# A QKV projection on one core: first row tiles loaded and turned one at a time, and a reordered last pair

## The chip, the core and the metric

The kernel runs on one core of one Trainium2 chip. The metric is device time in microseconds (us) of one execution. A profile is taken of one execution; its own clock counts from the start of the span, and its span is about 1.8 us shorter than the time that is reported for the run.

In the views of the profile, PE is TensorE (PEld its loading of weights), ACT is ScalarE, DVE is VectorE, POOL is GpSimd and SP is SyncE; a q behind a name marks the part of the engine that issues transfers, and L141 is line 141 of that run's kernel. To turn rows is to transpose them, to cast them is to convert them to bf16.

The kernel before takes 362.96 us (median of six runs, 362.75 to 363.25, taken in the rounds of the changed kernel). Each later group of experiments has runs of the kernel before on the same chip; their medians lie between 362.75 and 362.89.

## The reference

```python
x = randn(16, 512, 768)          # float32: 8192 rows of 768
w_qkv = randn(768, 2304)
qkv = np.matmul(x, w_qkv)
q, k, v = qkv[..., :768], qkv[..., 768:1536], qkv[..., 1536:]
return np.stack([q, k, v], axis=0).astype(np.float32)   # 75.5 MB out
```

## The kernel before

A "pair" is two row tiles of 128 rows. There are 32 pairs. Pairs 3 to 31 are done by a scheme of seven products with sums of blocks (`do(u, 1)` to `do(u, 7)`) on two groups of 1024 columns, and directly on the 256 columns that remain (`rem`). The scheme needs sums of weight blocks, which aren't there at the start, so pairs 0 to 2 are done directly in bf16, block by block of 512 columns. For these the rows are cast, turned on TensorE (six 128 by 128 transposes a row tile) and copied back. The change touches this start and the last pair. Cuts are marked by `...`.

```python
def load_rows(p):                                   # one transfer of 768 KB for a pair
    xin[p] = xin_pool.tile([P, 2, K], fp32, name="xin")
    rows = x_flat[p * 2 * P:(p + 1) * 2 * P, :]
    nc.sync.dma_start(xin[p][:], rows.rearrange("(r m) k -> m r k", m=P))

def copy_halves(dst, src, two):                     # VectorE, and ScalarE where two
    ...
def cast_rows(p, two=True):                         # both rows of a pair to bf16
    src = xin.pop(p)
    xc[p] = s_pool.tile([P, 2, K], bf16, name="xc", tag="s")
    for r in range(2):
        halves = (slice(0, K // 2), slice(K // 2, K))
        copy_halves([xc[p][:, r, n] for n in halves], [src[:, r, n] for n in halves], two)
def turn_rows(p, two=True):                         # both rows of a pair
    ...
            for j in range(KT):
                nc.tensor.transpose(ps[:, j, :], cols[:, j, :], eye)
    ...
# the last pair, a and b being the two groups of columns
    do(a, 1); do(b, 1); do(a, 2); do(a, 6); do(b, 2); do(b, 6)     # (one to a line)
    ...
    do(b, 4)
    store_cols(b, 1, 0, CB, nc.scalar)
    for u in (a, b):
        do(u, 3)
        store_cols(u, 0, CB, 2 * CB, nc.sync)
    rem_stored(1)
# the start: the loads, all on SyncE's queue, in this order
load_rows(0)
...
load_rows(1)
load_blocks(0, 0, 1)                                # six weight blocks of 256 KB
st_rem = o_pool.tile([P, KT, REM], fp32, name="str", tag="o")
load_w(st_rem[:], 0, KT, R_OFF, REM)                # the remainder's weights
load_rows(2)
load_blocks(0, 1)
...
# the start: the work
busy(11)                                            # products of zeros, the warm-up
cast_rows(0)
turn_rows(0)
busy(4)
cast_rows(1)
cast_k(0)                                           # a weight block to bf16
cast_k(1)
turn_rows(1)
...
block(0, 0, b1[0], singles, nothing)                # 24 products, pairs 0 and 1
rem(0)
rem(1)
cast_rows(2, False)
turn_rows(2, False)
block(0, 0, b1[0], halves((4, 5)), nothing)         # 12 products, pair 2
```

## Time and profile before

| | kernel before |
|---|---|
| time, median of six runs | 362.96 us |
| span of the profiled run | 361.4 us |
| landings: first pair, second pair, third pair | 5.05, 7.03, 15.31 us |
| first real product | 9.19 us |
| first product of the next weight block | 20.54 us |
| one repeated pair | 10.74 us |
| TensorE's end, last landing | 356.87, 360.04 us |

TensorE is busy almost all of the span (353.3 of 361.4 us), so the reader should look at two things only: when dense products begin, and what follows the last of them. The middle is the same in both kernels. The prediction below shows the lines of the page, of the timeline at both ends and of three windows. This is the kernel before in windows of 1 us; in each line the last three numbers are the granted clock, the share of the 16 DMA engines' time that is busy, and GB/s.

```profile
4.00:5.00 1.00, 1.00 (x3) 0.30 (x2) 0.00 (x0) 0.00 (x0) 0.00 (x0) 1.00 1.01 406
6.00:7.00 1.00, 1.00 (x14) 0.91 (x13) 0.33 (x1) 0.01 (x1) 0.00 (x0) 1.00 1.03 400
```

In both windows the DMA engines are full (shares of 1.01 and 1.03), at 400 GB/s and more. (The clock column reads 1.00 also where the trace has no record of the clock. In this run the record gives full speed only from 6.43 us, so in the first microseconds the spacing of the products tells the clock, and this column does not.)

### The profile page before, as it was taken

To read this page: it belongs to the slowest core of one execution; us is meant where nothing else is said; L and a number is where in the kernel's file an instruction comes from. 1 tells how busy PE (TensorE), PEld (TensorE's weight loads), DVE (VectorE), ACT (ScalarE), POOL (GpSimd) and SP (SyncE) were. 2 spreads that over 40 slices of the span, in tenths; PEclk is the share of its full clock that TensorE was granted. 3 is DMA by queue.
4 is the path that set the end of the run, shared out by engine and by line. 5 is a ranking of instruction groups with operands and counts; after the bars stand their busy time and mean duration, and the time that the engine had idled before them with its cause. 6 is when DMAs were issued, how large, how long until landed. Compare 5 with 4: busy or idle time off the path is not lost.

```text
span 361.4 us, 5220 instructions
## 1 busy us (share of the span) xinstructions
PE 353.3 (98%) x1765; PEld 250.8 (69%) x1797; DVE 222.7 (62%) x239; ACT 182.5 (51%) x304; POOL 174.4 (48%) x180
## 2 busy tenths in 40 slices
PE   8999999999999999999999999999999999999994
PEld 3644577777777777777777777777777777777763
DVE  3489546666566765566675565676556676556642
ACT  4547555455454545454545444445545454545452
POOL 0000970566664445664445665444666444566410
PEclk9999999999999999999999999999999999999999
DMA  7999969799899989999999999898999998989766
GB/s 294 381 383 338 348 227 345 271 354 304 279 322 298 296 275 296 282 313 314 284 278 295 282 306 316 284 276 291 295 285 317 295 296 276 297 279 331 267 251 242
DMA packets 80617, 108.08 MB, mean 299 GB/s; under 512 B 4816, under 2 KB 60368, under 8 KB 80592
## 3 DMA queue, kind: packets, MB, share of 16 engines
q1 hardware_dynamic: 65184, 96.35, 82.3%
q10 hardware_dynamic: 15408, 11.41, 9.9%
q8 instruction: 14, 0.23, 0.3%
q14 instruction: 11, 0.09, 0.1%
HBM read 32.24 MB, written 75.50 MB: 298 GB/s over the span
## 4 chain that ended last, share of the span: by engine, by line
PE 96%; ACT 1%; issue 1%; ACTq 0%; DVE 0%
PE ps L206 75%; PE ps L256 11%; PE ps L382 9%; PE ps L362 1%; PE ps L161 1%; ACT o L237 0%; ACTq L297 0%; ACT xb L141 0%; ACT orem L311 0%; DVE xb L139 0%; ACT xc L141 0%; ACTq L313 0%; DVE zero L340 0%; ACTq L311 0%
## 5 line engine op out<-in xcount | busy, mean ns | idle before, releaser
L206 PE MATMUL ps<-t,s 128*128 128x512 f32 x696 | 173.8, 398 | 0.0
L206 PEld LDWEIGHTS ps<-t,s 128*128 128x128 f32 x696 | 130.7, 188 | 29.8
L169 POOL CAST xb<-xf 128x1536 bf16<-128x1536 f32 x29 | 46.4, 1601 | 167.7 <-DVE xf L124 167.7
L234 DVE TENSOR_TENSOR o<-o,ps 128x512 f32<-128x512 f32 x58 | 39.9, 688 | 87.6 <-ACT o L233 87.6
L124 DVE STREAM_TRANSPOSE xf<-xin 128x1536 f32<-128x1536 f32 x29 | 85.7, 2956 | 9.7 <-DMA xin<-in_x_dram 7.1
L206 PE MATMUL ps<-b,xb 128*128 128x512 bf16 x320 | 82.4, 380 | 1.5
L233 ACT ACTIVATE o<-ps 128x512 f32<-128x512 f32 x58 | 34.7, 598 | 44.3 <-PE ps L206 44.3
L206 PEld LDWEIGHTS <-xb 128*128 128x128 bf16 x348 | 31.7, 98 | 35.6 <-issue 7.6
L227 ACT ACTIVATE o<-ps 128x512 f32<-128x512 f32 x58 | 34.8, 600 | 40.0 <-PE ps L206 37.3
L240 DVE TENSOR_TENSOR o<-o,ps 128x512 f32<-128x512 f32 x58 | 39.9, 688 | 21.4 <-PE ps L206 20.2
L206 PE MATMUL ps<-b,s 128*128 128x512 f32 x174 | 48.7, 389 | 0.0
L256 PE MATMUL ps<-w_rem,xb 128*128 128x256 bf16 x384 | 47.2, 273 | 0.0
L237 ACT ACTIVATE o<-ps 128x512 f32<-128x512 f32 x58 | 34.7, 598 | 24.1 <-PE ps L206 21.3
L220 ACT ACTIVATE o<-ps 128x512 f32<-128x512 f32 x58 | 34.6, 597 | 23.8 <-DVE o L240 20.7
L256 PEld LDWEIGHTS <-xb 128*128 128x128 bf16 x384 | 37.4, 98 | 11.2 <-issue 0.5
L224 DVE TENSOR_TENSOR o<-o,ps 128x512 f32<-128x512 f32 x58 | 36.5, 673 | 3.4 <-PE ps L206 2.1
L206 PEld LDWEIGHTS ps<-b,s 128*128 128x128 f32 x174 | 32.7, 188 | 6.8
L178 POOL TENSOR_TENSOR s<-s,xf 128x384 fp32r<-128x384 f32 x29 | 29.5, 1016 | 2.3
L266 ACT ACTIVATE orem<-ps 128x512 f32<-128x512 f32 x31 | 18.6, 598 | 22.7 <-PE ps L256 21.4
L179 POOL TENSOR_TENSOR s<-xf 128x384 fp32r<-128x384 f32 x29 | 29.5, 1017 | 0.0
L181 POOL TENSOR_TENSOR s<-xf,s 128x384 fp32r<-128x384 f32 x29 | 29.4, 1015 | 0.0
L177 POOL TENSOR_TENSOR s<-xf 128x384 fp32r<-128x384 f32 x29 | 29.3, 1012 | 0.0
(36 smaller groups left out, 127.2 us busy)
## 6 DMA issues: line engine op xcount, KB each, us to landing
out_dram<-o SPq DMA_DIRECT2D x62, 768.0 KB, 5.1
out_dram<-o SPq DMA_DIRECT2D x65, 256.0 KB, 4.6
xin<-in_x_dram SPq DMA_DIRECT2D x62, 192.0 KB, 6.7
xin<-in_x_dram ACTq DMA_DIRECT2D x54, 192.0 KB, 4.5
out_dram<-orem SPq DMA_DIRECT2D x31, 256.0 KB, 5.5
st<-in_w_qkv_dram SPq DMA_DIRECT2D x6, 768.0 KB, 14.1
xin<-in_x_dram SPq DMA_DIRECT2D x3, 768.0 KB, 5.8
st<-in_w_qkv_dram SPq DMA_DIRECT2D x6, 256.0 KB, 6.3
```

Of the source, the lines that this page charges most:

```text
L124: nc.vector.transpose(t[:].rearrange("p j (g b) -> p g j b", b=G), xin.pop(p)[:].rearrange("p g (a j) -> p g j a", a=G),)
L169: nc.gpsimd.tensor_copy(out=xb[p][:], in_=xf[p][:])
L206: nc.tensor.matmul(ps[:], lhs[j], rhs[j], start=(start and j == 0), stop=(j == KH - 1), skip_group_check=True,)
L220: nc.scalar.activation(c11, u.x[:], ident)
L224: nc.vector.tensor_tensor(c11, c11, u.z[:], op=add)
L227: nc.scalar.activation(c12, u.x[:], ident)
L233: nc.scalar.activation(c22, u.x[:], ident)
L234: nc.vector.tensor_tensor(c22, c22, u.y[:], op=add)
L237: nc.scalar.activation(c21, u.x[:], ident)
L240: nc.vector.tensor_tensor(c12, c12, u.y[:], op=add)
L256: nc.tensor.matmul(ps, xb[p][:, j, r * P:(r + 1) * P], w_rem[:, j, :], start=(j == 0), stop=(j == KT - 1), skip_group_check=True,)
L382: nc.tensor.matmul(ps[n][:], xb[p][:, j, r * P:(r + 1) * P], w[:, j, :], start=(j == 0), stop=(j == KT - 1), skip_group_check=True,)
```

## The change

Its intent has three parts. The first pair is loaded, cast and turned as two single rows, so that TensorE can do useful turning among the warm-up products; the second pair is to be turned sooner, its fourth row inside the first block. The third pair's two rows are turned one after each of the two remainder groups. In the last pair the remainder goes ahead of the last two products, and the last store is cut in two. The diff, cut to its core:

```diff
+    def load_row(p, r):
+        if r == 0:
+            xin[p] = xin_pool.tile([P, 2, K], fp32, name="xin")
+        row = (2 * p + r) * P
+        nc.sync.dma_start(xin[p][:, r, :], x_flat[row:row + P, :])
 ...                                  # cast_rows, turn_rows become cast_row, turn_row (p, r)
 ...                                  # last pair
         do(a, 4)
-        store_cols(a, 1, 0, CB, nc.scalar)
+        store_cols(a, 1, 0, CB, nc.sync)
+        do(a, 3)
+        store_cols(a, 0, CB, 2 * CB, nc.sync)
         rem_stored(0)
+        rem_stored(1)
         do(b, 4)
-        store_cols(b, 1, 0, CB, nc.scalar)
-        for u in (a, b):
-            do(u, 3)
-            store_cols(u, 0, CB, 2 * CB, nc.sync)
-        rem_stored(1)
+        store_cols(b, 1, 0, CB, nc.sync)
+        product(b, 3, b.y, False)
+        for lo in (CB, CB + CB // 2):
+            hi = lo + CB // 2
+            part = b.o[:, 0, lo:hi]
+            nc.vector.tensor_tensor(part, part, b.y[:, lo - CB:hi - CB], op=add)
+            store_cols(b, 0, lo, hi, nc.scalar)
 ...                                  # the start: loads
-    load_rows(0)
+    load_row(0, 0)
 ...
+    load_row(0, 1)
     load_rows(1)
 ...                                  # remainder weights in two halves
 ...                                  # the start: work
-    busy(11)
-    cast_rows(0)
-    turn_rows(0)
-    busy(4)
-    cast_rows(1)
+    busy(8)
+    cast_row(0, 0)
+    cast_row(0, 1)
+    turn_row(0, 0)
+    busy(1)
+    turn_row(0, 1)
+    busy(5)
+    cast_row(1, 0)
+    cast_row(1, 1)
     cast_k(0)
 ...                                  # fourth row turned as fourth_row() inside the first block
-    rem(0)
-    rem(1)
-    cast_rows(2, False)
-    turn_rows(2, False)
+    for p in range(2):
+        rem(p)
+        cast_row(2, p, False)
+        turn_row(2, p, False)
```

More of the change, by code (lines that the diff above doesn't have):

```diff
@@ L145, with cast_row, turn_row @@
     xc = {}
-    def cast_rows(p, two=True):
-        src = xin.pop(p)
-        xc[p] = s_pool.tile([P, 2, K], bf16, name="xc", tag="s")
-        for r in range(2):
-            halves = (slice(0, K // 2), slice(K // 2, K))
-            copy_halves([xc[p][:, r, n] for n in halves], [src[:, r, n] for n in halves], two)
-    def turn_rows(p, two=True):
-        c = xc.pop(p)
-        xb[p] = xb_pool.tile([P, KT, 2 * P], bf16, name="xb")
-        for r in range(2):
-            cols = c[:, r, :].rearrange("m (p j) -> m j p", j=KT)
-            ps = ps_pool.tile([P, KT, P], bf16, name="ps")
-            for j in range(KT):
-                nc.tensor.transpose(ps[:, j, :], cols[:, j, :], eye)
-            ks = (slice(0, KH), slice(KH, KT))
-            copy_halves(
-                [xb[p][:, n, r * P:(r + 1) * P] for n in ks], [ps[:, n, :] for n in ks], two
-            )
+    def cast_row(p, r, two=True):
+        if r == 0:
+            xc[p] = s_pool.tile([P, 2, K], bf16, name="xc", tag="s")
+        halves = (slice(0, K // 2), slice(K // 2, K))
+        copy_halves([xc[p][:, r, n] for n in halves], [xin[p][:, r, n] for n in halves], two)
+    def turn_row(p, r, two=True):
+        if r == 0:
+            xb[p] = xb_pool.tile([P, KT, 2 * P], bf16, name="xb")
+        cols = xc[p][:, r, :].rearrange("m (p j) -> m j p", j=KT)
+        ps = ps_pool.tile([P, KT, P], bf16, name="ps")
+        for j in range(KT):
+            nc.tensor.transpose(ps[:, j, :], cols[:, j, :], eye)
+        ks = (slice(0, KH), slice(KH, KT))
+        copy_halves(
+            [xb[p][:, n, r * P:(r + 1) * P] for n in ks], [ps[:, n, :] for n in ks], two
+        )
     def round_x(p):
@@ L313, in rem_stored @@
             nc.scalar.dma_start(out_flat[1, row:row + P, R_OFF - H:R_OFF - H + REM], o[:, 0, :])
-        do(a, 1)
-        do(b, 1)
-        do(a, 2)
-        do(a, 6)
-        do(b, 2)
-        do(b, 6)
+        for n in (1, 2):
+            for u in (a, b):
+                do(u, n)
         for u in (a, b):
             store_cols(u, 0, 0, CB, nc.sync)
-        for u in (a, b):
-            do(u, 5)
-            do(u, 7)
-            store_cols(u, 1, CB, 2 * CB, nc.sync)
+        do(a, 6)
+        do(a, 5)
+        do(b, 6)
+        do(a, 7)
+        store_cols(a, 1, CB, 2 * CB, nc.sync)
+        do(b, 5)
+        do(b, 7)
+        store_cols(b, 1, CB, 2 * CB, nc.sync)
         do(a, 4)
-        store_cols(a, 1, 0, CB, nc.scalar)
+        store_cols(a, 1, 0, CB, nc.sync)
+        do(a, 3)
+        store_cols(a, 0, CB, 2 * CB, nc.sync)
         rem_stored(0)
+        rem_stored(1)
         do(b, 4)
-        store_cols(b, 1, 0, CB, nc.scalar)
-        for u in (a, b):
-            do(u, 3)
-            store_cols(u, 0, CB, 2 * CB, nc.sync)
-        rem_stored(1)
+        store_cols(b, 1, 0, CB, nc.sync)
[5 more added lines that the diff above has]
+            store_cols(b, 0, lo, hi, nc.scalar)
     NS = 3
@@ L346, with load_k @@
     make_identity(nc, eye)
+    st_0 = tq_pool.tile([P, KT, CB], fp32, name="st0", tag="tq")
+    stage[0, 0, 0], stage[0, 1, 0] = st_0[:, :KH, :], st_0[:, KH:, :]
+    def load_k(j):
+        load_w(st_0[:, j:j + 1], j, 1, Q_OFF[0], CB)
+    load_row(0, 1)
     load_rows(1)
-    load_blocks(0, 0, 1)
+    for j in range(KT):
+        load_k(j)
     st_rem = o_pool.tile([P, KT, REM], fp32, name="str", tag="o")
-    load_w(st_rem[:], 0, KT, R_OFF, REM)
+    for h in range(2):
+        load_w(st_rem[:, h * KH:(h + 1) * KH], h * KH, KH, R_OFF, REM)
     load_rows(2)
-    load_blocks(0, 1)
+    load_blocks(0, 1, KH)
     load_blocks(1, 0)
@@ L375, in block @@
         ps = {}
-        for js, tiles in groups:
+        for group in groups:
+            if callable(group):
+                group()
+                continue
+            js, tiles = group
             for n in tiles:
@@ L396, in halves @@
         return [(range(h * KH, (h + 1) * KH), tiles) for h in range(2)]
-    singles = [((0, ), (0, 1)), ((1, ), (0, 1)), ((0, 1), (2, 3))]
-    singles += [((j, ), range(4)) for j in range(2, KT)]
     act, dve = nc.scalar, nc.vector
-    def cast_k(j):
-        dve.tensor_copy(out=b1[0][:, j, :], in_=stage[0, j // KH, 0][:, j % KH, :])
     def cast_next(q, c, w):
@@ L412, with fourth_row @@
     nothing = lambda p: None
-    busy(11)
-    cast_rows(0)
-    turn_rows(0)
-    busy(4)
-    cast_rows(1)
-    cast_k(0)
-    cast_k(1)
-    turn_rows(1)
-    for j in range(2, KT):
-        cast_k(j)
-    act.activation(w_rem[:, KH:], st_rem[:, KH:], ident)
-    dve.tensor_copy(out=w_rem[:, :KH], in_=st_rem[:, :KH])
+    busy(8)
[7 more added lines that the diff above has]
+    cast_row(1, 1)
+    cast_k(0)
+    turn_row(1, 0)
+    def fourth_row():
+        cast_k(1)
+        turn_row(1, 1)
+        for j in range(2, KT):
+            cast_k(j)
+        for h in range(2):
+            ks = slice(h * KH, (h + 1) * KH)
+            dve.tensor_copy(out=w_rem[:, ks], in_=st_rem[:, ks])
     bt0 = bt_pool.tile([P, KT, CB], bf16, name="bt")
     bt1 = bt_pool.tile([P, KT, CB], bf16, name="bt")
-    block(0, 0, b1[0], singles, nothing)
-    rem(0)
-    rem(1)
-    cast_rows(2, False)
-    turn_rows(2, False)
-    block(0, 0, b1[0], halves((4, 5)), nothing)
+    block(
+        0, 0, b1[0],
+        [((0, ), (0, 1)), fourth_row, ((1, ), (0, 1)), ((0, 1), (2, )), ((0, 1), (3, ))]
+        + [((j, ), range(4)) for j in range(2, KT)],
+        nothing,
+    )
+    for p in range(2):
+        rem(p)
+        cast_row(2, p, False)
+        turn_row(2, p, False)
+    block(0, 0, b1[0], [(range(KT), (4, )), (range(KT), (5, ))], nothing)
     for h in range(2):
```

## The prediction

> **What bounds the kernel now.** I read the page first (busy shares, the chain that ended last), then the chain in order of time at both ends, then the timeline, the transfers and windows of one microsecond there. The middle needs no more than the page:
>
> ```profile
> PE 353.3 (98%) x1765; PEld 250.8 (69%) x1797; DVE 222.7 (62%) x239; ACT 182.5 (51%) x304; POOL 174.4 (48%) x180
> PE 96%; ACT 1%; issue 1%; ACTq 0%; DVE 0%
> ```
>
> TensorE is busy for 353.3 of 361.4 us and is 96% of the chain. In the timeline its only gaps over 0.06 us are 1.19 at the start, 0.57 at 8.40, and 0.12 at 17.94; a repeated pair takes 10.74 us with one gap of 0.05. The change leaves the 28 repeated pairs alone, so it can win only in the 1.19 + 0.69 us of gaps, in warm-up work that is not the program's own, and in what follows TensorE's end. So I read the two ends. First the start, by the timeline (start, duration, instruction, and in brackets the idle time before it and who ended it):
>
> ```profile
> 1.19 4.88 PE L362 MATMUL ps<-zero 128*128 128x512 bf16 x11 [1.19 <-DVE zero L340]
> 5.08 0.94 ACT L141 ACTIVATE xc<-xin 128x384 bf16<-128x384 f32 x2 [2.85 <-DMA xin<-in_x_dram]
> 8.40 0.95 PE L161 MATMUL ps<-eye,xc 128*128 128x128 bf16 x12 [0.57 <-ACT xc L141]
> ...
> 9.19 5.34 PE L382 MATMUL ps<-b,xb 128*128 128x512 bf16 x23
> 14.37 2.78 PE L256 MATMUL ps<-w_rem,xb 128*128 128x256 bf16 x24
> 15.43 0.36 DVE L139 CAST xc<-xin 128x384 bf16<-128x384 f32 x1 [1.50 <-DMA xin<-in_x_dram]
> 16.99 0.83 PE L161 MATMUL ps<-eye,xc 128*128 128x128 bf16 x12
> 17.94 2.33 PE L382 MATMUL ps<-b,xb 128*128 128x512 bf16 x9
> ```
>
> The reader is to see two things: real products start at 9.19 and run densely; and the third pair of row tiles reaches VectorE only at 15.43, brought by a transfer, while TensorE reaches its turn at 16.99. So TensorE comes only about 0.9 us after that data can be turned (two casts, 15.43 to 16.06). The transfers are the second limit there:
>
> ```profile
> 8.00:9.00 1.00, 0.60 (x9) 0.58 (x10) 0.69 (x3) 0.76 (x2) 0.00 (x0) 1.00 1.05 387
> 12.00:13.00 1.00, 1.00 (x6) 0.49 (x5) 0.00 (x0) 0.00 (x0) 0.00 (x0) 1.00 1.12 373
> 14.00:15.00 1.00, 1.00 (x9) 0.71 (x8) 0.00 (x0) 1.00 (x3) 0.00 (x0) 1.00 1.04 399
> ```
>
> The last two columns are the DMA share (full) and GB/s. From about 2.6 us on the queue has no hole. The trace's landing marks: first pair 5.05, second 7.03, the six weight blocks 7.72, 8.38, 9.05, 9.73, 10.41, 11.09, the remainder weights 13.35, third pair 15.31. The end, again by the timeline:
>
> ```profile
> 355.56 1.37 DVE L240 TENSOR_TENSOR o<-o,ps 128x512 f32<-128x512 f32 x2 [1.42 <-PE ps L206]
> 356.04 0.83 PE L256 MATMUL ps<-w_rem,xb 128*128 128x256 bf16 x6
> 357.01 0.38 ACT L311 ACTIVATE orem<-ps 128x256 f32<-128x256 f32 x1 [0.97 <-PE ps L256]
> 357.42 0.34 ACTq L313 DMA_DIRECT2D out_dram<-orem  x1
> ```
>
> TensorE ends at 356.87; the last store, issued at 357.42, has its landing mark at 360.04, 2.62 us later, though another of the same 128 KB issued at 352.80 took 1.71. The 0.9 us more is queueing: the transfers run full from 354.95 to 359.56. From the last landing to the end of the span are 1.35 us of closing semaphores, which no part of the change touches.
>
> [...]Here they are full, so splitting brings the first piece early but not the last byte: the trace agrees by its share of 1.04 to 1.12.[...]the 11 warm-up products start 0.43 us apart, the four after 6.8 us 0.22.[...]
>
> **The change part by part.**
> *First rows singly.* Half of the first pair's 1.97 us of transfer can be used earlier: first row at about 5.05 - 0.98 = 4.07, second at 5.05. ScalarE's cast is 0.52, so the first row is turned from about 4.66, just as 8 warm-up products (1.19 + 8 x 0.43 = 4.6) end; the second after a ninth, near 5.7. All this hides: the second pair still lands at 7.03, is cast by 7.6, and the third row can be turned from 7.62. Its first half-cast weight block is ready at 7.74 + 0.42 = 8.16, against a first product at 9.19 before. The fourth row's turning (6 x 0.055 = 0.33) now lies inside the block. So 24 products of 0.216 and that 0.33 run from about 8.2 to 13.7; before they ended at 14.37. **Gain here: 0.67 us.**
> *Remainder weights in halves, both cast by VectorE.* The first half lands near 12.2, the last as before at 13.35, cast by 13.93. Three products of 0.11 come before it is needed, so TensorE loses nothing; the 0.85 us cast leaves ScalarE, which is no bound.
> *Third pair turned between the remainder products.* First remainder product group (12 x 0.109 = 1.31) 13.70 to 15.01. Then the in-order TensorE needs row five: no byte is moved earlier, so VectorE still casts from 15.43, by 16.06, and turning starts at about 16.10. **Lost: a wait of about 1.1 us.** After it: turn 0.33, second remainder group 1.31, about 0.08 for the sixth row's cast, turn 0.33, 12 products 2.59, all 4.64, to 20.74. The same point was 20.54 before (the next block's first product). **Start in sum: 0.2 us slower.** The 0.67 won is eaten by the wait, and the old order's overlap of both groups with the landing is given up. Later blocks follow TensorE: second-half weights (cast by 21.83) are needed 3.9 us after the block's start. So 0.2 passes through.
> *Last pair.* Same 54 matmuls (14 products of 3, and 12 of the remainder), another order: TensorE's duration is equal. Each dependence has room: product 3 of the first half needs its c22 add, some 1.55 us after product 7 (drain 0.17, copy 0.60, add 0.69, hops), and three products of 0.65 (3 x 0.216) lie between. After TensorE's end T, before: 0.14 + 0.38 + 0.03, issue at T + 0.55, landed T + 3.17.[...] What is left to store at T hardly changes (about 0.9 MB both times), but the two remainder stores are ahead of it and the last two pieces are small; filling a queue of 0.335 MB/us with the issues in order gives T + 2.98. **Gain 0.2 to 0.5, I take 0.35.**
> *Sum:* 362.89 + 0.2 - 0.35 = 362.74, rounded to 362.7.
>
> **The rivals.**
> 1. *The whole 0.67 us and more is kept* (third pair lands early enough, by about 14.3). For it: TensorE does get there sooner. Against: the same bytes precede it in a full queue. It would make 361.8.
> 2. *Clock stays low longer*[...] Against: the 1.1 us wait for the third pair would absorb most of it. It makes 362.8 to 363.5.
> 3. *The tail gives nothing or costs*[...]. If the transfers' queue drains the same bytes at the same rate, the end is unchanged: 363.1.
>
> **Range and chances.** The movable parts are below 1 us each, so 2% (7.3 us) is out of reach unless something breaks. Start between -0.7 and +0.6, tail between -0.5 and +0.2, runs of before spread over 0.26: 361.7 to 363.7. Faster by over 2% 1%, slower 1%.
>
> **What would show each step.** Right: in the new timeline first product near 8.2; the end of the first 24 near 13.7; a TensorE gap of about 1 us before the fifth row's transposes, released by VectorE's cast, itself released by the third pair's transfer near 15.4; the second weight block's first product near 20.7; the middle's pair still 10.74 us; last landing 2.7 to 3.0 us after TensorE's end. Wrong: a third pair landing clearly before 15 us, no such gap, warm-up products still 0.43 us apart after 7 us, or new TensorE gaps in the last pair.

The sum came to 362.74 us. The gain of 0.35 us at the tail: its ground is the estimate of 0.335 MB/us for the rate of the stores (the windows of before from 355 to 359 us show 292 to 379 GB/s). Rival 2: its 362.8 to 363.5 is an estimate whose ground was not shown.

Where the text says that "they are full", it means the DMA engines. Two things that it tells without a number can be read in the traces. A split did bring the first piece early and the last byte hardly: the changed kernel's first two rows landed at 3.74 and 4.85 us, where the pair had landed at 5.05. And TensorE did keep to the program's order: in the changed kernel it stood idle for 0.93 us ahead of the fifth row (17.80), and the second remainder group, whose rows and weights were ready by 15.62, came only after that row, at 18.18.

## The result, and the profile after

The changed kernel takes 364.99 us (median of six runs, 363.71 to 365.77), against 362.96 us. The ratio is 1.0053, with a 95% interval of 1.0036 to 1.0071. A ratio here is the mean time of one kernel's fast runs over the mean of the other's in the same rounds, so it is not quite the quotient of the medians. The change costs about 2.0 us by the medians: within 2%, but slower, and outside the predicted range of 361.7 to 363.7.

The page of the changed kernel, busy shares and the chain that ended last:

```profile
PE 353.6 (97%) x1764; PEld 251.1 (69%) x1796; DVE 225.3 (62%) x241; ACT 182.4 (50%) x303; POOL 174.0 (48%) x180
PE 93%; DMA 4%; issue 1%; SPq 0%; DVE 0%; DVEq 0%
```

TensorE's busy time is as it was (353.6 against 353.3 us). What is new is DMA in the chain, with 4%, where before there was none. The timeline of the changed kernel (start, duration, instruction, idle time before it and who ended it) shows where:

```profile
8.72 0.94 ACT L147 ACTIVATE xc<-xin 128x384 bf16<-128x384 f32 x2 [1.31 <-DMA xin<-in_x_dram]
9.30 0.54 PE L165 MATMUL ps<-eye,xc 128*128 128x128 bf16 x6 [1.45 <-ACT xc L147]
9.89 0.59 PE L406 MATMUL ps<-b,xb 128*128 128x512 bf16 x2
...
17.80 0.54 PE L165 MATMUL ps<-eye,xc 128*128 128x128 bf16 x6 [0.93 <-DVE xc L149]
```

There are two holes in TensorE. The first, 1.45 us, is ahead of the turn of the third row: ScalarE casts that row at 8.72, and the cast was released by a transfer, the second pair's. The second, 0.93 us, is ahead of the fifth row, as predicted in kind. That it is near the predicted 1.1 us is luck, since both of its ends had moved: the remainder's products began at 15.40 in place of 13.70, and the third pair landed 1.68 us late. The chain of waits of the changed kernel, in order of time (start, duration, what), says the same from the other side:

```profile
2.12 7.27 DMA st<-in_w_qkv_dram
9.39 0.02 issue
9.40 7.59 DMA xin<-in_x_dram
...
17.48 0.28 DVE xc L149
17.80 0.54 PE ps L165 x6
```

Up to 17 us the chain runs through two transfers, the first weight block and the third pair. Before, it ran through TensorE from 8.40 us on, but for 0.4 us of VectorE at 17.53. The landings in both traces, in us:

| landing | before | after | difference |
|---|---|---|---|
| first pair | 5.05 | rows 3.74 and 4.85 | |
| second pair | 7.03 | 8.70 | +1.67 |
| first weight block | 7.72 | 9.39 | +1.67 |
| sixth weight block | 11.09 | 12.80 | +1.71 |
| third pair | 15.31 | 16.99 | +1.68 |

The first pair comes a little earlier than predicted (4.07 and 5.05). The second pair comes 1.67 us late, although the bytes ahead of it in the queue and its own are the same, and every later landing up to the third pair is late by about as much (1.66 to 1.71 us). The windows of the changed kernel for the same time:

```profile
4.00:5.00 1.00, 1.00 (x6) 0.55 (x5) 0.24 (x2) 0.41 (x2) 0.00 (x0) 1.00 0.86 289
5.00:6.00 1.00, 1.00 (x9) 0.74 (x8) 0.59 (x2) 0.55 (x2) 0.00 (x0) 1.00 0.95 347
6.00:7.00 1.00, 1.00 (x7) 0.59 (x6) 0.36 (x1) 0.43 (x2) 0.00 (x0) 1.00 0.89 289
```

The share falls from 1.01 to 0.86 and the rate from 406 to 289 GB/s, in the windows right after the first row's landing. The trace has 16 landing marks for each transfer. For the second pair's they are, in us:

```
before  6.47 6.63 6.64 6.66 6.67 6.68 6.70 6.82 6.84 6.88 6.89 6.91 6.92 7.00 7.01 7.03
after   6.37 6.38 6.44 6.47 6.50 6.56 6.58 6.62 6.73 6.76 6.86 7.14 7.31 7.79 7.89 8.70
```

Eleven of the sixteen marks, each taken here as the end of one part of the transfer, come by 6.86, none later than those of before, and five come later than any of before, the last by 1.67 us. So the mean rate is not the whole story: the casts of the pair began at 8.72 us, right after the sixteenth mark at 8.70, and not after the fifteenth at 7.89. (The trace does not say which engine a packet or a mark belongs to.)

At the end, the changed kernel's timeline is:

```profile
358.03 0.86 PE L210 MATMUL ps<-b,s 128*128 128x512 f32 x3
...
358.93 0.75 DVE L344 TENSOR_TENSOR o<-o,ps 128x256 f32<-128x256 f32 x2 [2.04 <-PE ps L210]
359.38 0.82 ACTq L301 DMA_DIRECT2D out_dram<-o  x2
```

TensorE ends at 358.89 and the last landing is at 362.11, so 3.22 us after TensorE's end. Before it was 3.17 us. The tail has given nothing. In the middle a repeated pair still takes 10.74 us.

### The profile page after: what moved, and what is told of

It reads as the page before. It is cut to its first block, busy times and chain, and to the rows that moved or that the text cites. A ratio compares the mean times of both kernels' runs of the same rounds, so it can differ in the third digit from the quotient of the medians.

```text
span 363.3 us, 5223 instructions
## 1 busy us (share of the span) xinstructions
PE 353.6 (97%) x1764; PEld 251.1 (69%) x1796; DVE 225.3 (62%) x241; ACT 182.4 (50%) x303; POOL 174.0 (48%) x180
## 4 chain that ended last, share of the span: by engine, by line
PE 93%; DMA 4%; issue 1%; SPq 0%; DVE 0%; DVEq 0%
PE ps L210 75%; PE ps L260 11%; PE ps L406 7%; DMA xin<-in_x_dram 2%; DMA st<-in_w_qkv_dram 2%; PE ps L165 0%; SPq L136 0%; SPq L141 0%; DVE o L344 0%; DVE xc L145 0%; DVEq L523 0%; DVE xc L149 0%; DVEq L145 0%
## 5 line engine op out<-in xcount | busy, mean ns | idle before, releaser
L173 POOL CAST xb<-xf 128x1536 bf16<-128x1536 f32 x29 | 43.9, 1514 | 170.0 <-DVE xf L124 170.0
L181 POOL TENSOR_TENSOR s<-xf 128x384 fp32r<-128x384 f32 x29 | 30.9, 1064 | 0.0
L183 POOL TENSOR_TENSOR s<-xf 128x384 fp32r<-128x384 f32 x29 | 29.5, 1017 | 0.0
```

The lines of the kernel that those rows point to most:

```text
L173: nc.gpsimd.tensor_copy(out=xb[p][:], in_=xf[p][:])
L181: g.tensor_tensor(s[:, 1], a21, a22, op=add)
```

## The experiments

The theory after the first comparison was: the loss is at the start, and it is the splitting of the first load into two short transfers, whatever the engines do with the rows. The rivals were that the tail costs something, that the new order of turning costs it (the wait for the third pair), and that the new warm-up leaves the clock low.

| run | what it is | us (before, same rounds) | ratio, 95% interval | second / third pair landed | first product / next block |
|---|---|---|---|---|---|
| e1_tail_only | before, new tail | 362.73 (362.80) | 0.9999, 0.9988–1.0011 | 7.02 / 15.30 | 8.78 / 20.15 |
| e2_start_only | after, old tail | 365.58 (362.80) | 1.0072, 1.0059–1.0085 | 8.69 / 17.50 | 9.88 / 23.07 |
| e3_pair0 | after, first pair in one transfer | 363.36 (362.80) | 1.0017, 1.0005–1.0029 | 6.96 / 15.24 | 8.46 / 20.81 |
| e4_split0 | before, first pair split by rows | 364.35 (362.80) | 1.0047, 1.0030–1.0063 | 9.15 / 17.44 | 10.54 / 23.62 |
| e5_split0_late | e4, casts wait for both rows | 364.46 (362.75) | 1.0038, 1.0025–1.0051 | 8.69 / 16.95 | 10.08 / 21.82 |
| e6_cols0 | before, first pair split by columns | 363.38 (362.75) | 1.0021, 1.0005–1.0037 | 7.43 / 16.00 | 8.87 / 20.86 |
| e7_split1 | before, second pair split by rows | 362.88 (362.75) | 1.0000, 0.9987–1.0013 | 7.30 / 15.55 | 8.74 / 20.42 |
| e8_pair0_rem | e3, both remainder groups first | 364.26 (362.75) | 1.0033, 1.0020–1.0047 | 6.93 / 15.21 | 10.02 / 21.96 |
| e9_pair0_warm | e3, old warm-up | 363.39 (362.89) | 1.0012, 1.0000–1.0025 | 7.01 / 15.29 | 8.36 / 20.86 |
| e10_pair0_warm_rem | e9, both remainder groups first | 362.78 (362.89) | 1.0001, 0.9987–1.0015 | 6.97 / 15.25 | 8.33 / 20.19 |
| e11_split01 | before, both pairs split by rows | 363.85 (362.89) | 1.0026, 1.0012–1.0039 | 8.39 / 16.71 | 9.58 / 21.57 |
| e12_split0_act | e4, second row on ScalarE's queue | 362.49 (362.77) | 0.9993, 0.9978–1.0008 | 6.79 / 15.06 | 8.42 / 19.92 |
| e13_split0_alt | e4, even rows then odd rows | 364.37 (362.77) | 1.0046, 1.0029–1.0062 | 8.77 / 17.07 | 10.16 / 21.93 |
| e14_pair6k | before, first pair in pieces of 6 KB | 363.07 (362.77) | 1.0009, 0.9994–1.0024 | 6.99 / 15.33 | 9.48 / 20.83 |

The times are of four to six runs each; the landings and first products are those of one profiled execution.

### Start or tail: e1 and e2

e1 is the kernel before with the whole new `last()`; e2 is the changed kernel with the whole old `last()`, so its edit is that of e1 backwards. The edit of e1, cut to its core:

```diff
 # e1, from before.py
-        do(b, 4)
-        ...
-        rem_stored(1)
+        rem_stored(1)
+        do(b, 4)
+        ...
+        product(b, 3, b.y, False)          # and its add and store in two halves
```

> The kernel before with the new order of the last pair alone. In the changed kernel the last landing mark came 3.22 us after TensorE's end, before it was 3.17. Theory A (the last pair gives nothing, the queue of stores sets its end): within 0.2 us of the kernel before, ratio 0.9995 to 1.0005. My prediction's step (gain of 0.2 to 0.5 us): ratio about 0.999.

> The changed kernel with the old last pair. Theory A (all of the loss is at the start): as slow as the changed kernel, about 364.5 to 365, ratio 1.004 to 1.006, and the second pair's landing mark again late, 8 us or later, against 7.03 before. Rival (the last pair costs part of it): ratio under 1.003.

e1 took 362.73 us against 362.80: no gain to be seen. Its interval would still hold the predicted gain of 0.35 us, so the times alone don't rule it out; the traces below do. e2 took 365.58 us: all of the loss. It is even 0.59 us above the changed kernel, but not by its tail: its profiled run is 0.50 us longer (365.58 against 365.08), and its next block had begun 0.51 us later already (23.07 against 22.56). The timeline of e1 at its end is the same sequence as that of the changed kernel:

```profile
355.60 0.86 PE L206 MATMUL ps<-b,s 128*128 128x512 f32 x3
...
356.95 0.82 ACTq L297 DMA_DIRECT2D out_dram<-o  x2
```

TensorE ends at 356.46. The last store of all is issued at 357.38, so 0.92 us after TensorE's end (before it was 0.55), and lands at 359.66, 3.20 us after TensorE's end. It is shorter in flight than the last store of before (2.28 against 2.62 us), but is issued later by as much. The prediction had the queue drained at 2.98 us after TensorE's end; it took 0.22 us more. All sixteen traces have the last landing 3.14 to 3.22 us after TensorE's end, the six with the new tail (3.19 to 3.22) no earlier than the ten with the old one. The packets that started after TensorE's end carry 0.93 MB in before and 0.90 MB in e1. That the bytes still to be stored decide, and not when the last of them is issued, fits this; no run varied those bytes.

### Is it the split? e3, e4 and e5

e3 gives the changed kernel its first pair in one transfer again. e4 is the opposite: it does the split alone, in the kernel before. e5 is e4 with the casts taking the second row first, so no engine touches the rows until both have landed.

```diff
 # e3, from after.py
-    load_row(0, 0)
+    load_rows(0)
 ...
-    load_row(0, 1)
 # e4, from before.py
-    load_rows(0)
+    xin[0] = xin_pool.tile([P, 2, K], fp32, name="xin")
+    for r in range(2):
+        nc.sync.dma_start(xin[0][:, r, :], x_flat[r * P:(r + 1) * P, :])
 # e5, from e4, in cast_rows
-        for r in range(2):
+        for r in (1, 0) if p == 0 else (0, 1):
```

> The changed kernel with the first pair loaded by one transfer of 768 KB again, all else kept. Theory A (two single-row transfers of 384 KB at the head of the queue[...] the second pair lands 1.7 us late): second pair lands near 7.0, third near 15.3, TensorE gap before the fifth row's transposes about 1 us, next block's first product near 20.7 to 20.8, time 362.9 to 363.3. Rival B (the early casts and the other order of computing slow the transfers): second pair still lands at 8 or later, time as the changed kernel's.

> The kernel before with only the first pair's load split in two single-row transfers. Theory A: second pair's landing mark moves from 7.03 to 8 or later, and with it all later ones; TensorE waits for it, time up by 0.8 to 2 us (363.8 to 365). Rival B (the split is harmless, the order of computing is the cause): landing near 7.0, time unchanged within 0.2 us.

> The kernel before with the first pair loaded by two single-row transfers, as in the run before this, but the second row is cast first, so that no engine computes on x before both have landed, as before. Theory A (the transfers alone are the cause): second pair still lands at 8 us or later, ratio 1.003 to 1.006. Rival B (computing on the first row while the next transfers run is what slows them): second pair lands near 7.0, ratio 1.000.

e3 took 363.36 us. Its second pair landed at 6.96 and its third at 15.24. The timeline of e3 shows a start that ends as predicted, within 0.1 us:

```profile
8.46 0.59 PE L405 MATMUL ps<-b,xb 128*128 128x512 bf16 x2
...
16.06 0.54 PE L165 MATMUL ps<-eye,xc 128*128 128x128 bf16 x6 [0.43 <-DVE xc L149]
...
20.81 3.40 PE L405 MATMUL ps<-bt,xb 128*128 128x512 bf16 x15
```

The next block begins at 20.81 (predicted 20.74) and the fifth row is turned at 16.06 (predicted 16.10). On the way there it is not as predicted: the remainder's products begin at 14.15 and not at 13.70, and the wait for the fifth row is 0.43 us and not 1.1. The two differences cancel, since the third pair's landing sets the time of the turn. Taking the split away gives back 364.99 - 363.36 = 1.63 us of the 2.03 lost; the two are from different rounds, with the kernel before at 362.96 and 362.80.

e4 took 364.35 us: the split by itself costs 1.55 us by the medians. Its timeline:

```profile
9.17 0.94 ACT L141 ACTIVATE xc<-xin 128x384 bf16<-128x384 f32 x2 [2.31 <-DMA xin<-in_x_dram]
9.75 0.95 PE L161 MATMUL ps<-eye,xc 128*128 128x128 bf16 x12 [2.98 <-ACT xc L141]
10.54 7.07 PE L384 MATMUL ps<-b,xb 128*128 128x512 bf16 x24
```

TensorE stands idle for 2.98 us until the second pair is cast, which landed at 9.15. The 24 products then take 7.07 us where the same 24 took 5.34 in e1. The trace's clock record says why: half clock from 11.06 to 14.47, so for 3.41 us after the long hole. This was the slowest of e4's six runs (366.15); the others lie between 363.63 and 364.86. The slowest run of the changed kernel (365.77) may have had the same: its mean granted clock is 0.993, as in this run, and 0.998 to 1.000 in the other five. No trace of it was kept.

e5 took 364.46 us with the second pair at 8.69. Its casts began at 4.76 us, when both rows had landed, as in the kernel before (5.08). So casting and turning a single row early is not what slows the transfers. The transfers do it by themselves.

### What about the split? e6, e7, e11, e13 and e14

These change one property of the first transfers each. e6 cuts the pair by columns (two transfers of 256 pieces of 1.5 KB). e7 splits the second pair instead of the first. e11 splits both, so that four short transfers come first and the second short one is not followed by a long one. e13 takes two transfers of the same size, but even rows and then odd rows (a wrong result, as the output's rows are then permuted). e14 is one transfer of half as many pieces, each two rows long (wrong too).

```diff
-    load_rows(0)
+    xin[0] = xin_pool.tile([P, 2, K], fp32, name="xin")
 # e6
+    for h in range(2):
+        cs = slice(h * K // 2, (h + 1) * K // 2)
+        nc.sync.dma_start(
+            xin[0][:, :, cs], x_flat[:2 * P, cs].rearrange("(r m) k -> m r k", m=P)
+        )
 # e13
+    for r in range(2):
+        alternate = x_flat[:2 * P, :].rearrange("(m r) k -> m r k", r=2)
+        nc.sync.dma_start(xin[0][:, r, :], alternate[:, r, :])
 # e14
+    nc.sync.dma_start(xin[0][:], x_flat[:2 * P, :].rearrange("(m r) k -> m r k", r=2))
 # e7 in place of load_rows(1) alone; e11 so, and the split of e4
+    for r in range(2):
+        nc.sync.dma_start(xin[1][:, r, :], x_flat[(2 + r) * P:(3 + r) * P, :])
```

> The kernel before with the first pair cut in two transfers of 384 KB by columns, each of both rows (256 pieces of 1.5 KB in place of 128 of 3 KB). Theory A1 (a short transfer at the head of the queue is the cause, whatever its shape): second pair lands at 8 or later, ratio 1.003 to 1.006. Theory A2 (it is the few long pieces[...] of the single-row form): second pair lands near 7.0, ratio 1.000.

> The kernel before with the second pair, not the first, loaded by two single-row transfers. Theory A3 (only the head of the queue is sensitive): fourth row lands near 7.0, weights and third pair as before (third 15.3), ratio 1.000. Rival (single-row transfers of this form fall behind anywhere): first weight block lands at 8.5 or later against 7.72, third pair after 16, ratio 1.002 to 1.005.

> The kernel before with the first and the second pair both loaded in single rows, four transfers of 384 KB. Theory A1 (short single-row transfers at the head of the queue[...]): fourth row lands at 8 or later, ratio 1.003 to 1.006. Theory A4[...]: fourth row lands near 7.0 to 7.3, ratio 1.000 to 1.001.

> Wrong result on purpose (the first 256 rows are permuted): the kernel before with the first pair in two transfers of 128 rows, the even rows and then the odd ones[...]. Theory R (the addresses an engine reads in a row decide): second pair lands near 7.0, ratio 1.000. Theory P or Q (the form of the transfers): 8 or later, ratio 1.003 to 1.006.

> Wrong result on purpose (the first 256 rows are permuted): the kernel before with the first pair still in one transfer of 768 KB, but two neighbouring rows to a partition, so 128 pieces of 6 KB in place of 256 of 3 KB. Theory P (few pieces[...] at the head): second pair lands at 8 or later, ratio 1.003 to 1.006. Theory Q (it takes two transfers): near 7.0, ratio 1.000.

e7 cost nothing that can be seen (362.88 us against 362.75). Its second pair was 0.27 us late and its third 0.24 (15.55 against 15.31), so a split behind the head does much less harm. e13 lost as much as e4 (364.37 us), so it does not matter whether a transfer reads neighbouring rows or every other one. e14 came out at 363.07 us, with the second pair at 6.99, on time, so few pieces alone don't do it. (The clock became full only at 7.13 in its profile, which puts its first product at 9.48.) e11 lost 1.0 us with its fourth row at 8.39, so a step from short transfers to a long one (from 128 pieces to 256, its theory A4) isn't needed. e6 lay between (363.38 us, second pair at 7.43): neither of the two expected results. Two short transfers in line do less harm here in pieces of 1.5 KB; why was not tested.

The trace also has a record of each single packet, with its queue but not its engine. These packets started 4 to 8 us after the start of the span, in the profiled runs; the mean in flight is the sum of their durations over the 4 us:

| run | mean packets in flight | packets over 200 ns | longest, ns | second pair landed |
|---|---|---|---|---|
| before | 16.5 | 0 | 174 | 7.03 |
| e3_pair0 | 16.6 | 0 | 186 | 6.96 |
| after | 14.8 | 31 | 645 | 8.70 |
| e4_split0 | 14.9 | 32 | 1011 | 9.15 |
| e5_split0_late | 15.1 | 25 | 1313 | 8.69 |
| e13_split0_alt | 15.9 | 21 | 1075 | 8.77 |
| e11_split01 | 14.8 | 28 | 1304 | 8.39 |
| e2_start_only | 15.9 | 4 | 547 | 8.69 |
| e7_split1 | 16.0 | 13 | 619 | 7.30 |
| e6_cols0 | 16.6 | 5 | 679 | 7.43 |
| e12_split0_act | 16.5 | 4 | 293 | 6.79 |

A usual packet of 3 KB takes 121 ns. In five of the six runs with the pair split by rows at the head of one queue, 21 to 32 packets take more than 200 ns, up to eleven times the usual. But e2, whose start is the changed kernel's, has only four packets over 200 ns and the same late landing. And the last packets of the late parts are not slow themselves: in the changed kernel the last six of the second pair take 121 to 124 ns each and follow one another from 7.66 to 8.38 us. So slow packets go with the delay in most runs, and are not shown to be what makes it.

### One queue or two: e12

e12 keeps the two short transfers and issues the second from ScalarE.

```diff
 # from e4
-        nc.sync.dma_start(xin[0][:, r, :], x_flat[r * P:(r + 1) * P, :])
+        (nc.sync, nc.scalar)[r].dma_start(xin[0][:, r, :], x_flat[r * P:(r + 1) * P, :])
```

> The kernel before with the first pair in two single-row transfers, the second of them issued by ScalarE, so that both run side by side. Theory Q (two short transfers in line in one queue are needed): second pair lands near 7.0, ratio 1.000. Theory P (128 pieces of 3 KB in a transfer[...] are enough wherever they queue): second pair at 8 or later, ratio 1.003 to 1.006.

The delay is gone. The second pair's marks end at 6.79, the third pair lands at 15.06, and the next block begins at 19.92. The windows of e12, to be held against the two of before:

```profile
4.00:5.00 1.00, 1.00 (x4) 0.40 (x3) 0.29 (x2) 0.29 (x1) 0.00 (x0) 1.00 1.02 403
6.00:7.00 1.00, 1.00 (x9) 0.38 (x6) 0.77 (x3) 0.74 (x2) 0.00 (x0) 1.00 1.04 398
```

So the same bytes in the same two pieces cost nothing where they are in two queues (362.49 us against 362.77). The trace has the two transfers in two queues, issued at 0.73 us by ScalarE and at 0.74 by SyncE, and in the windows the engines are full (shares of 1.02 and 1.04), at 403 and 398 GB/s. It does not show what happens inside an engine, so why two short transfers in line cost time and two in two queues do not was not shown.

A rival is the time of issue, since ScalarE issues the second row while SyncE issues the first, and so the second pair is issued at 1.19 us and not at 1.65 as in e4. But these are 0.46 us, and the landing moved by 2.36 us (9.15 to 6.79). e6 issued its second pair still later than e4 (1.74 us) and had it earlier (7.43 us).

e12 is also the fastest version: 362.49 us, with three of its four runs (362.45, 362.47, 362.51, 362.79) below every run of before in its rounds (362.69 to 363.06). But the ratio of 0.9993 has an interval of 0.9978 to 1.0008, which holds 1. It is as fast as before, and perhaps 0.1% faster.

### The order of the remainder: e8, e9 and e10

e3 still lost about 0.56 us. The prediction had put 1.1 us down to the wait for the third pair. e8 is e3 with both remainder groups ahead of the third pair's turn, as before the change.

```diff
 # e8, from e3
-    for p in range(2):
-        rem(p)
-        cast_row(2, p, False)
-        turn_row(2, p, False)
+    for p in range(2):
+        rem(p)
+    for r in range(2):
+        cast_row(2, r, False)
+    for r in range(2):
+        turn_row(2, r, False)
 # e9, from e3; e10 is e9 with the edit of e8 as well
-    busy(8)
+    busy(11)
     cast_row(0, 0)
     cast_row(0, 1)
     turn_row(0, 0)
-    busy(1)
     turn_row(0, 1)
-    busy(5)
+    busy(4)
```

> The changed kernel with the first pair in one transfer, and both remainder products ahead of the third pair's casts and turns, as in the kernel before. My prediction's step (TensorE waits about 1 us for the fifth row in the changed order, while the second remainder group stands behind it): that gap shrinks below 0.4 us, next block's first product moves from 20.81 to about 19.9, ratio to the kernel before 0.9975 to 0.999, so about 0.9 us under the run with the pair alone. Rival (the wait only moves to the copies of the turned rows): next block's first product stays above 20.4, ratio 1.000 to 1.002.

> The changed kernel with the first pair in one transfer and the old warm-up (11 products ahead of the first transposes, 4 after them), still with the third pair turned between the remainder products. Theory C (with 8 warm-up products TensorE idles 0.8 us before the first transposes[...]): warm-up gap gone, clock full by 6.5, first product near 8.2 to 8.5, next block's first product 20.7 to 20.8, ratio 1.001 to 1.002. Rival: first product at 10 in the profile again, ratio 1.003.

> The same with both remainder products ahead of the third pair's casts and turns. My prediction's step (the changed order costs about 0.9 us) with theory C: first product 8.2 to 8.5, next block's first product 19.8 to 20.0, time 362.1 to 362.5, ratio 0.998 to 0.9993, and 0.8 to 0.9 us under the kernel sent with it; it would then beat both kernels. Rival (the order of turning costs nothing): both kernels of this pair alike within 0.2 us.

e8 missed what was expected of it: 364.26 us, slower than e3. Its transfers are on time, but its timeline shows another cause:

```profile
5.54 0.84 PE L165 MATMUL ps<-eye,xc 128*128 128x128 bf16 x6 [0.76 <-ACT xc L147]
...
7.24 2.34 PE L380 MATMUL ps<-zero 128*128 128x512 bf16 x5
9.38 0.84 PE L165 MATMUL ps<-eye,xc 128*128 128x128 bf16 x6
10.02 0.85 PE L405 MATMUL ps<-b,xb 128*128 128x512 bf16 x2
```

Five warm-up products take 2.34 us, 0.43 us from one to the next, where in e3 the same five took 1.24. The clock record gives full speed only from 10.54 us, against 4.21 in e3 and between 4.2 and 7.2 in all other runs. (The clock column of the windows reads 1.00 there, as the trace has no record for that time; the spacing of products tells.) Five of e8's six runs took 364.0 to 364.6 us and one 362.87, so whatever it is comes and goes with the run. Only one of the six has a trace: that the low clock made the other four slow is likely, and not shown. e8 and e3 are the same program up to 14 us, so the edit itself, as far as any trace shows, has no means to act at 5 us. They ran on different chips (4 and 5); why e8 was slow so often is not settled. The low clock is the prediction's second rival, in a run where it was not looked for.

e9 and e10 take the old, denser warm-up, so that the order can be tested alone. (Theory C put e8's slow runs down to the idle time before its first transposes, 0.76 us, and a full clock that then comes late. That the one follows from the other was not shown: e3 stood idle there for 1.05 us and kept the full clock that it had from 4.21 us.) e9 took 363.39 us, as e3 did (363.36), so the thinner warm-up costs nothing in a usual run. It had the wait at the fifth row, 0.58 us. From e9's timeline:

```profile
16.11 0.54 PE L165 MATMUL ps<-eye,xc 128*128 128x128 bf16 x6 [0.58 <-DVE xc L149]
```

e10 took 362.78 us, with no wait there. From e10's timeline:

```profile
8.33 0.59 PE L405 MATMUL ps<-b,xb 128*128 128x512 bf16 x2
...
14.02 2.78 PE L260 MATMUL ps<-w_rem,xb 128*128 128x256 bf16 x24
16.64 0.83 PE L165 MATMUL ps<-eye,xc 128*128 128x128 bf16 x12
...
20.19 4.05 PE L405 MATMUL ps<-bt,xb 128*128 128x512 bf16 x18
```

The order alone is worth 363.39 - 362.78 = 0.61 us, and 0.67 us in the traces (20.86 against 20.19 for the next block). (e9's five runs took 363.33 to 363.42 us; four of e10's took 362.73 to 362.92 and one 363.48.) But e10, expected at 362.1 to 362.5, does not beat the kernel before (362.89 us, ratio 1.0001). The reason is in e1, whose start is that of the kernel before, word for word. From e1's timeline:

```profile
8.78 5.34 PE L388 MATMUL ps<-b,xb 128*128 128x512 bf16 x24
13.97 2.79 PE L256 MATMUL ps<-w_rem,xb 128*128 128x256 bf16 x24
...
20.15 3.19 PE L388 MATMUL ps<-bt,xb 128*128 128x512 bf16 x14
```

The remainder begins at 13.97 here and at 14.02 in e10. The profile of before that the prediction was made from had it at 14.37, with the first product at 9.19: its clock was full only at 6.43 us (4.92 in e1), and at 363.17 us it was a slow one: five of the six runs of the kernel before in the rounds of the changed kernel took less. So the 0.67 us that was to be won was measured from a late start. And e10's earlier first product (8.33 against 8.78) buys nothing, since the fourth row's turn and waits of 0.2 us now lie inside the block.

## Why the prediction was wrong

**The step that failed** is in the first part of the change: "All this hides: the second pair still lands at 7.03". The prediction took the queue for full and therefore the bytes' order for the only thing that counts. But two short transfers in line at its head left some of the second pair's sixteen parts behind, so that it landed late: 8.70 us in the changed kernel, 9.15 with the split alone (e4), 6.96 with the split taken away (e3), 6.79 with the second row on another queue (e12). Everything later in the queue was late by the same 1.7 us, the third pair included (16.99). Two further terms of the sum were mis-sized, the gain of 0.67 us and the wait of 1.1 us, and the gain of 0.35 us at the tail did not come.

Point by point:

- *First product near 8.2, end of the first 24 near 13.7:* wrong. They were 9.89 and 15.40. With the split undone, e3 and e10 had 8.46 and 8.33 for the first, 14.15 and 14.02 for the second, so the chain of casts and turns was about right; the end of the 24 was put 0.3 to 0.45 us too early.
- *A gain of 0.67 us:* mis-sized even without the split. It was measured from one profiled run with a late clock; against the start of e1 it is about 0.0 us (13.97 against 14.02).
- *A wait of about 1.1 us for the third pair:* right in kind, mis-sized. With the split undone it was 0.43 us (e3) and 0.58 us (e9), as the first 24 products ended later than predicted and so nearer to the third pair's landing. The 0.93 us of the changed kernel is near 1.1 by luck, and came at 17.80 in place of 16.10. That the order costs something is right: 0.61 us, e9 against e10.
- *Start in sum +0.2 us:* the next block began at 22.56, where 20.74 was predicted, so 1.82 us later.
- *The repeated pairs at 10.74 us:* right.
- *The tail gains 0.35 us:* wrong, it gained nothing (e1: 362.73 against 362.80 us, the last landing 3.20 us after TensorE's end against 3.17). Rival 3 said so and came true; its reason, that the same bytes drain at the same rate, fits the traces and was not tested. The two half adds took 0.42 and 0.41 us, together 0.83 where one whole add takes 0.69. The prediction had counted on about as much, so the size of the adds was not the mistake. The prediction read the transfers as full from 354.95 to 359.56 us; in the view there is a hole of about 0.15 us near 356.85, too small to matter.
- *Rival 2, the clock:* not the cause in the changed kernel, whose clock was full at 6.95 us, before its first product. It is what cost time in e8's profiled run. The prediction: in its trace the spacings of 0.43 and 0.22 us show a half and a full clock, and the half clock lasted from the first product at 1.19 to 6.43 us, so 5.2 us.

The two errors account for the miss. The predicted 362.74, with 1.82 us more at the start and 0.35 us less won at the end, makes 364.91; measured were 364.99. The 1.82 us hold the late transfers, the missing gain and the smaller wait together. By experiments: the split 1.63 us (e3), the order 0.61 us (e9 and e10), the tail nothing (e1).

**What stays open** is why two short transfers in line at the head of a queue make parts of the next transfer late. The runs rule out early work on the rows (e5), the order of the rows read (e13), few pieces as such (e14) and the step to a longer transfer (e11). They show that it takes one queue (e12), and that it is strong only at the queue's head (e7). Slow packets, of up to 1.3 us, go with it, but hardly in e2. A mechanism was not found.

## What to carry to other kernels

A full queue is not proof that cutting a transfer is free (here the cut alone cost 1.55 us, e4): when you cut one at the head of a queue, look at all of the landing marks of the transfer behind it, and if the last few trail, give the second piece to another queue (the landing moved from 9.15 to 6.79 us here). Size a gain against several runs of the kernel before, since a single profile can have a late clock, which moved the start by 0.4 us here. Where the queue is full, as here, try work that waits for a late transfer behind whatever else there is to do (0.61 us here, e9 against e10).
